# Gate/up with more seven-product k-pairs in each pair of chunks, token sums in smaller steps

## The chip, the cores and the metric

The kernel runs on one NeuronCore of a Trainium2 chip, as one launch. The metric is the time on the device in microseconds (us), as the median of several runs. A profiled execution of the same kernel gives the trace that the rows below come from. TensorE (PE) multiplies, VectorE (DVE) and ScalarE (ACT) do element work, SyncE (SP) issues the weight transfers, GpSimd (POOL) has little to do here.

## What is computed

The reference is a two-layer decoder trunk over 256 tokens of width 2048, in float32: a layer with dilated attention, a layer with sparse attention, and behind each a SwiGLU feed-forward. The change touches the first half of the feed-forward, in both layers.

```python
def swiglu(u, w_gu, w_down):
    gu = u @ w_gu
    return (jax.nn.silu(gu[..., :D_FF]) * gu[..., D_FF:]) @ w_down
# in reference(), per layer, D_FF = 5632:
x = x + rmsnorm(o, g[1])
x = x + rmsnorm(swiglu(rmsnorm(x, g[2]), ffn_w_gu[l], ffn_w_down[l]), g[3])
```

## The kernel before

**Splits.** TensorE multiplies numbers of reduced length, so that each float32 operand is cut into a high and a low part and a product takes three matmuls: high by high, low by high, high by low. `split_ap` makes the parts of a weight tile: ScalarE copies it to `hi` (L258), VectorE subtracts to get `lo` (L259). A weight unit is a tile of 128x1024, loaded by SyncE into `raw`.

**Gate/up.** The hidden width is done in 22 chunks, each with 8 units (one for each k-pair u, two blocks of 128 of the input width). Chunks go in 11 pairs, cp = 0 to 10. In pair 0 both chunks run side by side (`x_unit`, L425 to L427). In pairs 1 to 7 (`GU_PAIRS`) `gu_pair` runs them as a `Block7` (L465 to L467), in which some k-pairs, the "quads" (kind "S"), are computed with seven products instead of eight, a Strassen-like 2x2 scheme over two halves of the tokens, two k-blocks and two chunks. `_gu_quads` says which: u = 0 and 1 in even pairs, 0 to 2 in odd ones. Pairs 8 to 10 run chunk by chunk in the plain form. Two plain units of a k-pair take 24 matmuls, a quad 21.

A quad needs combined weights: of the first chunk's unit a and the second's b it takes a high and a low part of one half of b (`hl`, 128x512), T13 (two subtractions of 128x512, L274 and L275), T24 (two additions of 128x512 into the raw tile, L284 and L285), and splits of a, T13 and T24 of 128x1024. It also needs combined activations. `x_sums` makes them in the course of pair 0, for each u: `xw` adds high and low part (L1106), `sv` and `sx` (L1110 to L1116) are the four sums of a quad (`Sx`, for u < 3), `sv` and `ex` (L1121 to L1127) the differences for plain units within a Block7 (`Ex`, for u from 2 on).

**Evacuation.** When a pair is done, `evac` adds its accumulators (L509, L515), applies Silu and multiplies (L1159, L1160); for plain chunks `gu_evac` does it (L1088, L1090). Then `gu_split` transposes each hidden block f2 (L1068) and makes its high and low parts `hT` (L1072, L1073). Blocks f2 from 14 on (`DN_S`) have seven-product k-pairs in the down projection, and `s_parts` makes their four sums here, on ScalarE (`s` L1043, `hT` and `sp` L1059) and VectorE (`sv` L1046 to L1049, `hT` and `sp` L1060). Blocks 14 and 15 come from pair 7.

**What sets the order.** The program's order is the order of each engine's queue. `take` fetches the next unit: before it hands one out it issues loads and splits up to `st["look"]` units ahead, as long as `st["res"]` + 2 of the 48 SBUF pages (tiles of 128x1024) are free; where they aren't, the split comes when the unit is taken. Pages hold raw, hi, lo, X, the sums and the growing `hT`. The side work (`x_sums`, `gu_evac`, `sums`, `evac`) consists of generators that move on with the ticks of the products: `yield n` waits n ticks, and one plain unit gives 8 ticks.

```python
    def room(n):
        return len(pages.own) + len(pages.free) >= st["res"] + n
            # in take(), twice for each unit:
            if st["split"] < min(i + 1 + st["look"], n, ...) and room(2):
                split_one()
```

Of the kernel before, what the change touches and what calls it, by code (L numbers as in the profile page):

```python
# [18 lines left out]
S = 256  # L19
D = 2048  # L20
KT = D // P
HD = 128
DFF = 5632
FT = DFF // P
# [65 lines left out]

GU_PAIRS = range(1, 8)
GU_E = range(2, KT // 2)


def _gu_quads(cp):
    return tuple(range(2 + cp % 2))


def _gu_steps(cp):
# [5 lines left out]
def _gu_order(l):  # L107
    n, o = KT // 2, []
    for cp in range(FT // 4):
        if cp == 0:  # L110

            o += [(f"gu{l}", c * n + u) for u in range(n) for c in range(2)]
        elif cp in GU_PAIRS:
            o += _pair_order(f"gu{l}", n, cp, _gu_steps(cp))
        else:
            o += [(f"gu{l}", 2 * cp * n + u) for u in range(2 * n)]
    return o


# [100 lines left out]
def trunk(ctx: ExitStack, tc: tile.TileContext, a: dict, out: bass.AP):  # L220
# [858 lines left out]
    def gu_evac(f2, pts, H, rf, Sp):  # L1079

        while "r" not in rf:
            yield 0
        H.grow(f2)
        hs = []
        for t in range(2):
            r = rf["r"][:, t:t + 1]
            g = tmp.tile([P, S], F32, tag="ev1", name="ev1", bufs=2)
            nc.scalar.activation(g, pts[t][1][:, :S], AF.Silu, scale=r)  # L1088
            h = tmp.tile([P, S], F32, tag="ev2", name="ev2", bufs=2)
            nc.vector.scalar_tensor_tensor(h, pts[t][1][:, S:], r, g, op0=OP.mult, op1=OP.mult)  # L1090
            banks.put(pts[t][0])
            hs.append(h)
        yield 8
        yield from gu_split(f2, hs, H, Sp)

    def x_sums(X, Sx, Ex):

        e = None
        for u in range(KT // 2):
            while not X.done.issuperset((2 * u, 2 * u + 1)):  # L1100
                yield 0
            yield 6
            x = X.t[u][1].bitcast(F32)
            i, w = pages.get([P, 2, 2, P], F32, "xw")
            tt = nc.vector.tensor_tensor
            tt(out=w.rearrange("p k t q -> p k (t q)"), in0=x[:, :, 0, :], in1=x[:, :, 1, :], op=OP.add)  # L1106
            yield 2
            if u < 3:
                sv = tmp.tile([P, 4, P], F32, tag="sv", name="sv")
                tt(out=sv[:, 0], in0=w[:, 1, 1], in1=w[:, 0, 1], op=OP.add)  # L1110
                tt(out=sv[:, 1], in0=sv[:, 0], in1=w[:, 0, 0], op=OP.subtract)
                tt(out=sv[:, 2], in0=w[:, 0, 0], in1=w[:, 0, 1], op=OP.subtract)
                tt(out=sv[:, 3], in0=w[:, 1, 0], in1=sv[:, 1], op=OP.subtract)
                pg = pages.get([P, 4, 2, P], F32R, "sx")
                nc.scalar.activation(pg[1][:, :, 0, :], sv, AF.Copy)
                tt(out=pg[1][:, :, 1, :], in0=sv, in1=pg[1][:, :, 0, :].bitcast(F32), op=OP.subtract)  # L1116
                Sx[u] = {"pg": pg, "s": [[pg[1][:, j, k, :] for k in range(2)] for j in range(4)]}
                yield 2
            if u in GU_E:
                sv = tmp.tile([P, 4, P], F32, tag="sv", name="sv")  # L1120
                tt(out=sv[:, :2], in0=w[:, :, 0], in1=w[:, :, 1], op=OP.subtract)  # L1121
                at = (u - GU_E[0]) % 2 * 2
                if at == 0:
                    e = pages.get([P, 4, 2, P], F32R, "ex")
                    Ex[("pg", u)] = e
                nc.scalar.activation(e[1][:, at:at + 2, 0, :], sv[:, :2], AF.Copy)
                tt(out=e[1][:, at:at + 2, 1, :], in0=sv[:, :2], in1=e[1][:, at:at + 2, 0, :].bitcast(F32),  # L1127
                   op=OP.subtract)
                for k in range(2):
                    Ex[2 * u + k] = [e[1][:, at + k, j, :] for j in range(2)]  # L1130
            pages.put(i)

    def gu_pair(l, cp, X, Sx, Ex, H, Sp, rf):
# [12 lines left out]
        def evac():  # L1146
# [18 lines left out]
            for e in T["pg"]:  # L1165
                pages.put(e[0])

        for j, (kd, u) in enumerate(plan):
            blk.step(kd, u)
            if kd == "S" and all(e[0] != "S" for e in plan[j + 1:]):  # L1170
                spawn(sums())
        spawn(evac())

    def ffn(l, X, rf, gidx, step=lambda u: None, first=lambda c: None):
# [3 lines left out]
        spawn(x_sums(X, Sx, Ex))  # L1178
        for cp in range(FT // 4):
            if cp in GU_PAIRS:  # L1180
                st["res"], st["look"] = 5, 5
                gu_pair(l, cp, X, Sx, Ex, H, Sp, rf)
                continue
            if cp == GU_PAIRS[-1] + 1:
                st["spare"] = lambda: 2
                st["res"], st["look"] = 2, 4
                for e in Sx.values():
                    pages.put(e["pg"][0])
                for key, e in Ex.items():
                    if isinstance(key, tuple):  # L1190
                        pages.put(e[0])
            for fs in [(0, 1)] if cp == 0 else [(2 * cp,), (2 * cp + 1,)]:
                pts = [[bank(), bank()] for _ in fs]
                for u in range(KT // 2):
                    for p in pts:
                        x_unit(p, f"gu{l}", X, 2 * u, 512, u == 0, u == KT // 2 - 1, fs[0] == FT // 2 - 1)
                for f2, p in zip(fs, pts):
                    spawn(gu_evac(f2, p, H, rf, Sp))
        until(lambda: len(H.t) == FT // 2)
        X.release()  # L1200
        tail = Tail(gidx, "f")
        st["res"] = 4
# [92 lines left out]
    rf = {}  # L1295
# [412 lines left out]
```

## Time and profile before

| | |
|---|---|
| median of 3 runs | 2521.18 us (2521.03 to 2521.21) |
| profiled execution, time | 2519.93 us |
| its span | 2518.2 us |
| its mean granted clock of TensorE | 0.996 of full speed |
| gate/up, pairs 1 to 10, layer 1 | from about 1842 to 2284 us of the span |

A row of a timeline gives the start, the length, the engine, the line and what is written from what; the brackets at its end give the idle time of that engine just before and what ended it. Tiles stand without numbers there (`t` is T13). Matmuls are pipelined: a row's own length is longer than the distance to the next.

### The profile page before, as it was taken

To read this page: it belongs to the slowest core of one execution; us is meant where nothing else is said; L and a number is where in the kernel's file an instruction comes from. 1 tells how busy PE (TensorE), PEld (TensorE's weight loads), DVE (VectorE), ACT (ScalarE), POOL (GpSimd) and SP (SyncE) were. 2 spreads that over 40 slices of the span, in tenths; PEclk is the share of its full clock that TensorE was granted. 3 is DMA by queue.
4 is the path that set the end of the run, shared out by engine and by line. 5 is a ranking of instruction groups with operands and counts; after the bars stand their busy time and mean duration, and the time that the engine had idled before them with its cause. 6 is when DMAs were issued, how large, how long until landed. Compare 5 with 4: busy or idle time off the path is not lost. (4 is left out here: it accounts for less than half of the span.)

```text
span 2518.2 us, 32856 instructions
## 1 busy us (share of the span) xinstructions
PE 2478.4 (98%) x12122; PEld 2098.3 (83%) x12122; DVE 1859.0 (74%) x2638; ACT 1330.3 (53%) x1932; POOL 59.2 (2%) x74
## 2 busy tenths in 40 slices
PE   8999999999999999999999999999899999999998
PEld 7899999988788888888888888888778888888886
DVE  8565555557898878578897866896688987758796
ACT  7443444446555545455565566565455555545553
POOL 5000000000000000000000000000000000000000
PEclk9999999999999999999999999999999999999999
DMA  7555545576465546556586675346455655656664
GB/s 281 182 177 175 168 164 171 177 246 222 173 213 179 194 166 220 175 193 210 200 292 205 211 249 209 118 151 218 159 176 176 217 176 176 214 171 209 213 225 155
DMA packets 138529, 491.28 MB, mean 195 GB/s; under 512 B 15712, under 2 KB 15840, under 8 KB 138368
## 3 DMA queue, kind: packets, MB, share of 16 engines
q1 hardware_dynamic: 134208, 476.24, 55.4%
q0 software_dynamic: 3440, 11.83, 1.3%
q8 instruction: 95, 1.56, 0.3%
q10 hardware_dynamic: 720, 1.11, 0.1%
q14 instruction: 66, 0.54, 0.1%
HBM read 482.82 MB, written 6.29 MB: 194 GB/s over the span
## 5 line engine op out<-in xcount | busy, mean ns | idle before, releaser
L259 DVE TENSOR_TENSOR lo<-raw,hi 128x1024 fp32r<-128x1024 f32 (+2 forms) x899 | 1048.0, 1206 | 260.9 <-ACT hi L258 234.4
L258 ACT ACTIVATE hi<-raw 128x1024 fp32r<-128x1024 f32 (+2 forms) x899 | 889.7, 1035 | 153.2 <-PE bk L467 32.7
L390 PE MATMUL bk<-xT,hi 128*128 128x512 f32 x1104 | 399.2, 405 | 0.0
L392 PE MATMUL bk<-xT,lo 128*128 128x256 f32 x1035 | 289.8, 280 | 0.0
L390 PEld LDWEIGHTS bk<-xT,hi 128*128 128x128 f32 x1104 | 204.1, 188 | 39.9 <-issue 0.2
L465 PE MATMUL bk<-hi,hT 128*128 128x512 f32 x576 | 224.3, 389 | 0.0
L466 PE MATMUL bk<-hi,hT 128*128 128x512 f32 x576 | 224.1, 389 | 0.0
L467 PE MATMUL bk<-lo,hT 128*128 128x512 f32 x576 | 224.1, 389 | 0.0
L465 PE MATMUL bk<-hi,xf 128*128 128x512 f32 x564 | 222.4, 394 | 0.0
L467 PE MATMUL bk<-lo,xf 128*128 128x512 f32 x564 | 220.0, 390 | 0.0
L466 PE MATMUL bk<-hi,xf 128*128 128x512 f32 x564 | 219.9, 390 | 0.0
L427 PE MATMUL bk<-lo,xf 128*128 128x512 f32 x512 | 200.5, 392 | 3.2 <-DVE lo L259 3.2
L425 PE MATMUL bk<-hi,xf 128*128 128x512 f32 x512 | 202.5, 395 | 0.9 <-ACT xf L556 0.6
L426 PE MATMUL bk<-hi,xf 128*128 128x512 f32 x512 | 200.0, 391 | 0.0
L392 PEld LDWEIGHTS bk<-xT,lo 128*128 128x128 f32 x1035 | 195.5, 189 | 3.2
L258 ACT ACTIVATE hi<-t 128x1024 fp32r<-128x1024 f32 x68 | 72.3, 1063 | 192.6 <-DVE t L275 175.6
L465 PEld LDWEIGHTS bk<-hi,hT 128*128 128x128 f32 x576 | 108.1, 188 | 22.6
L467 PEld LDWEIGHTS bk<-lo,hT 128*128 128x128 f32 x576 | 108.1, 188 | 22.4
L466 PEld LDWEIGHTS bk<-hi,hT 128*128 128x128 f32 x576 | 108.1, 188 | 22.3
L467 PEld LDWEIGHTS bk<-lo,xf 128*128 128x128 f32 x564 | 106.0, 188 | 22.2
L465 PEld LDWEIGHTS bk<-hi,xf 128*128 128x128 f32 x564 | 106.2, 188 | 21.3
L466 PEld LDWEIGHTS bk<-hi,xf 128*128 128x128 f32 x564 | 106.3, 188 | 21.0
(301 smaller groups left out, 4210.0 us busy)
## 6 DMA issues: line engine op xcount, KB each, us to landing
raw<-in_gu SPq DMA_DIRECT2D x352, 512.0 KB, 4.1
raw<-in_dn SPq DMA_DIRECT2D x176, 512.0 KB, 4.3
raw<-in_a_qk SPq DMA_DIRECT2D x96, 512.0 KB, 3.3
raw<-in_a_v SPq DMA_DIRECT2D x64, 384.0 KB, 3.1
raw<-in_cw SPq DMA_DIRECT2D x32, 512.0 KB, 4.4
raw<-in_b_out SPq DMA_DIRECT2D x32, 512.0 KB, 3.8
raw<-in_a_out SPq DMA_DIRECT2D x24, 512.0 KB, 3.9
raw<-in_b_q SPq DMA_DIRECT2D x24, 512.0 KB, 3.3
```

The costliest lines, as they stand in the source:

```text
L258: nc.scalar.activation(hi, src, AF.Copy)
L259: nc.vector.tensor_tensor(out=lo, in0=src, in1=hi.bitcast(F32), op=OP.subtract)
L390: mm(pt[:, :], lhsT=hi[:, ks], rhs=X.hl(kt), start=first, stop=last)
L392: mm(pt[:, S:], lhsT=lo[:, ks], rhs=X.part(kt, 0), start=False, stop=False)
L425: mm(p[:, :w], lhsT=xh, rhs=u[0][1][:, ws], start=f, stop=False)
L426: mm(p[:, :w], lhsT=xl, rhs=u[0][1][:, ws], start=False, stop=False)
L427: mm(p[:, :w], lhsT=xh, rhs=u[1][1][:, ws], start=False, stop=l)
L465: mm(p, lhsT=xh, rhs=wh, start=f, stop=False)
L466: mm(p, lhsT=xl, rhs=wh, start=False, stop=False)
L467: mm(p, lhsT=xh, rhs=wl, start=False, stop=e)
```

## The change

`GU_PAIRS` now reaches to pair 10, with three quads in pairs 1 to 7 and two in pairs 8 to 10. The number of units that may be split ahead is 5 throughout; the pages held in reserve are 5 up to pair 7, then 4 and 3. `Sx[2]` is given back at pair 8. X, the sums and the differences are given back one by one inside pair 10; before, the sums and differences went at the start of pair 8. The steps of `x_sums` are drawn apart, `gu_evac` (pair 0 alone now) waits before its first step (1 tick for the first chunk, 17 for the second) and 14 instead of 8 ticks before the transposes. The last pair's evacuation falls into the start of the down projection.

```diff
@@ -90,12 +90,12 @@
 
 
 
-GU_PAIRS = range(1, 8)
+GU_PAIRS = range(1, 11)
 GU_E = range(2, KT // 2)
 
 
 def _gu_quads(cp):
-    return tuple(range(2 + cp % 2))
+    return tuple(range(3 if cp < 8 else 2))
 
 
 def _gu_steps(cp):
@@ -110,10 +110,8 @@
         if cp == 0:
 
             o += [(f"gu{l}", c * n + u) for u in range(n) for c in range(2)]
-        elif cp in GU_PAIRS:
+        else:
             o += _pair_order(f"gu{l}", n, cp, _gu_steps(cp))
-        else:
-            o += [(f"gu{l}", 2 * cp * n + u) for u in range(2 * n)]
     return o
 
 
@@ -1080,6 +1078,7 @@
 
         while "r" not in rf:
             yield 0
+        yield 1 + 16 * f2
         H.grow(f2)
         hs = []
         for t in range(2):
@@ -1090,7 +1089,7 @@
             nc.vector.scalar_tensor_tensor(h, pts[t][1][:, S:], r, g, op0=OP.mult, op1=OP.mult)
             banks.put(pts[t][0])
             hs.append(h)
-        yield 8
+        yield 14
         yield from gu_split(f2, hs, H, Sp)
 
     def x_sums(X, Sx, Ex):
@@ -1099,12 +1098,12 @@
         for u in range(KT // 2):
             while not X.done.issuperset((2 * u, 2 * u + 1)):
                 yield 0
-            yield 6
+            yield 4
             x = X.t[u][1].bitcast(F32)
             i, w = pages.get([P, 2, 2, P], F32, "xw")
             tt = nc.vector.tensor_tensor
             tt(out=w.rearrange("p k t q -> p k (t q)"), in0=x[:, :, 0, :], in1=x[:, :, 1, :], op=OP.add)
-            yield 2
+            yield 3
             if u < 3:
                 sv = tmp.tile([P, 4, P], F32, tag="sv", name="sv")
                 tt(out=sv[:, 0], in0=w[:, 1, 1], in1=w[:, 0, 1], op=OP.add)
@@ -1113,9 +1112,10 @@
                 tt(out=sv[:, 3], in0=w[:, 1, 0], in1=sv[:, 1], op=OP.subtract)
                 pg = pages.get([P, 4, 2, P], F32R, "sx")
                 nc.scalar.activation(pg[1][:, :, 0, :], sv, AF.Copy)
+                yield 3
                 tt(out=pg[1][:, :, 1, :], in0=sv, in1=pg[1][:, :, 0, :].bitcast(F32), op=OP.subtract)
                 Sx[u] = {"pg": pg, "s": [[pg[1][:, j, k, :] for k in range(2)] for j in range(4)]}
-                yield 2
+                yield 3
             if u in GU_E:
                 sv = tmp.tile([P, 4, P], F32, tag="sv", name="sv")
                 tt(out=sv[:, :2], in0=w[:, :, 0], in1=w[:, :, 1], op=OP.subtract)
@@ -1124,10 +1124,12 @@
                     e = pages.get([P, 4, 2, P], F32R, "ex")
                     Ex[("pg", u)] = e
                 nc.scalar.activation(e[1][:, at:at + 2, 0, :], sv[:, :2], AF.Copy)
+                yield 3
                 tt(out=e[1][:, at:at + 2, 1, :], in0=sv[:, :2], in1=e[1][:, at:at + 2, 0, :].bitcast(F32),
                    op=OP.subtract)
                 for k in range(2):
                     Ex[2 * u + k] = [e[1][:, at + k, j, :] for j in range(2)]
+                yield 3
             pages.put(i)
 
     def gu_pair(l, cp, X, Sx, Ex, H, Sp, rf):
@@ -1165,10 +1167,19 @@
             for e in T["pg"]:
                 pages.put(e[0])
 
+        st["res"], st["look"] = (5 if cp < 8 else 4 if cp == 8 else 3), 5
+        if cp == 8:
+            pages.put(Sx.pop(2)["pg"][0])
         for j, (kd, u) in enumerate(plan):
             blk.step(kd, u)
             if kd == "S" and all(e[0] != "S" for e in plan[j + 1:]):
                 spawn(sums())
+            if cp == GU_PAIRS[-1] and kd != "a":
+                X.drop_one(u)
+                if kd == "S":
+                    pages.put(Sx[u]["pg"][0])
+                elif u == KT // 2 - 1 or (u - GU_E[0]) % 2:
+                    pages.put(Ex[("pg", u - (u - GU_E[0]) % 2)][0])
         spawn(evac())
 
     def ffn(l, X, rf, gidx, step=lambda u: None, first=lambda c: None):
@@ -1178,25 +1189,15 @@
         spawn(x_sums(X, Sx, Ex))
         for cp in range(FT // 4):
             if cp in GU_PAIRS:
-                st["res"], st["look"] = 5, 5
                 gu_pair(l, cp, X, Sx, Ex, H, Sp, rf)
                 continue
-            if cp == GU_PAIRS[-1] + 1:
-                st["spare"] = lambda: 2
-                st["res"], st["look"] = 2, 4
-                for e in Sx.values():
-                    pages.put(e["pg"][0])
-                for key, e in Ex.items():
-                    if isinstance(key, tuple):
-                        pages.put(e[0])
-            for fs in [(0, 1)] if cp == 0 else [(2 * cp,), (2 * cp + 1,)]:
-                pts = [[bank(), bank()] for _ in fs]
-                for u in range(KT // 2):
-                    for p in pts:
-                        x_unit(p, f"gu{l}", X, 2 * u, 512, u == 0, u == KT // 2 - 1, fs[0] == FT // 2 - 1)
-                for f2, p in zip(fs, pts):
-                    spawn(gu_evac(f2, p, H, rf, Sp))
-        until(lambda: len(H.t) == FT // 2)
+            pts = [[bank(), bank()] for _ in range(2)]
+            for u in range(KT // 2):
+                for p in pts:
+                    x_unit(p, f"gu{l}", X, 2 * u, 512, u == 0, u == KT // 2 - 1)
+            for f2, p in enumerate(pts):
+                spawn(gu_evac(f2, p, H, rf, Sp))
+        st["spare"] = lambda: 2
         X.release()
         tail = Tail(gidx, "f")
         st["res"] = 4
```

In all, TensorE's instructions go from 11611 to 11557 in the program.

VectorE, layer 1, where the last plain chunks are computed. Before, behind the transposes of block 20 (`hT`), four `sv` and the `hT` and `sp` of its sums are followed by splits of plain units, of which several are already done:

```order
L259 TENSOR_TENSOR lo_3002_19492<-raw_2993_19430,hi_3001_19491 128x1024
L1073 TENSOR_TENSOR hT_3000_19473<-sk_506_19500,hT_3000_19473 128x2x256
L1046 TENSOR_TENSOR sv_19512<-sk_506_19500,s11_19510 128x128
L1047 TENSOR_TENSOR sv_19512<-sv_19512,sk_506_19500 128x128
L1048 TENSOR_TENSOR sv_19512<-sk_506_19500,s11_19510 128x128
L1049 TENSOR_TENSOR sv_19512<-sk_506_19500,sv_19512 128x128
L1060 TENSOR_TENSOR hT_3000_19473<-sv_19512,hT_3000_19473 128x128
L1060 TENSOR_TENSOR sp_2979_19345<-sv_19512,sp_2979_19345 128x128
L1060 TENSOR_TENSOR sp_3004_19517<-sv_19512,sp_3004_19517 128x2x128
L259 TENSOR_TENSOR lo_3006_19531<-raw_2996_19448,hi_3005_19530 128x1024
```

Now, at the entry of pair 10 in layer 1, the end of the second of two such chains (blocks 18 and 19), and then the splits of the pair's first quad:

```order
L1046 TENSOR_TENSOR sv_19697<-sk_521_19685,s11_19695 128x128
L1047 TENSOR_TENSOR sv_19697<-sk_521_19685,sv_19697 128x128
L1058 TENSOR_TENSOR hT_3070_19639<-sv_19697,hT_3070_19639 128x128
L1058 TENSOR_TENSOR sp_3073_19680<-sv_19697,sp_3073_19680 128x128
L1058 TENSOR_TENSOR sp_3074_19702<-sv_19697,sp_3074_19702 128x2x128
L257 TENSOR_TENSOR hl_3076_19724<-raw_3065_19598,hl_3076_19724 128x512
L272 TENSOR_TENSOR t13_3077_19727<-raw_3065_19598,raw_3062_19580 128x512
L273 TENSOR_TENSOR t13_3077_19727<-raw_3065_19598 128x512
L282 TENSOR_TENSOR raw_3062_19580<-t13_3077_19727,raw_3062_19580 128x512
L283 TENSOR_TENSOR raw_3062_19580<-raw_3062_19580 128x512
L257 TENSOR_TENSOR lo_3080_19737<-t13_3077_19727,hi_3079_19736 128x1024
L257 TENSOR_TENSOR lo_3082_19751<-raw_3062_19580,hi_3081_19750 128x1024
```

The splits that stand behind the sums (`hl`, T13, T24) were plain `lo` before, of units further ahead.

TensorE at the same two places. Before, behind the transposes come plain units whose parts (`hi_3014`, `lo_3015`) were split long ahead:

```order
L1068 MATMUL sk_509_19676<-cst_70,ev2_19652 128x128
L1068 MATMUL sk_509_19676<-cst_70,ev2_19656 128x128
L1068 MATMUL sk_509_19676<-cst_70,ev2_19652 128x128
L1068 MATMUL sk_509_19676<-cst_70,ev2_19656 128x128
L425 MATMUL bk_508_19639<-hi_3014_19584,xf_2400_15826 128x512
L426 MATMUL bk_508_19639<-hi_3014_19584,xf_2400_15826 128x512
L427 MATMUL bk_508_19639<-lo_3015_19585,xf_2400_15826 128x512
L425 MATMUL bk_507_19638<-hi_3014_19584,xf_2400_15826 128x512
L426 MATMUL bk_507_19638<-hi_3014_19584,xf_2400_15826 128x512
```

Now, from the tenth matmul behind the second transposes of pair 10, the last products of the quad's unit a, then those with `hl` and T13 (`hi_3079`, `lo_3080`):

```order
L463 MATMUL bk_522_19717<-hi_3071_19673,xf_2441_15921 128x512
L464 MATMUL bk_522_19717<-hi_3071_19673,xf_2441_15921 128x512
L465 MATMUL bk_522_19717<-lo_3072_19674,xf_2441_15921 128x512
L463 MATMUL bk_518_19600<-hi_3071_19673,xf_2441_15921 128x512
L464 MATMUL bk_518_19600<-hi_3071_19673,xf_2441_15921 128x512
L465 MATMUL bk_518_19600<-lo_3072_19674,xf_2441_15921 128x512
L463 MATMUL bk_523_19732<-hl_3076_19724,sx_2462_16105 128x512
L464 MATMUL bk_523_19732<-hl_3076_19724,sx_2462_16105 128x512
L465 MATMUL bk_523_19732<-hl_3076_19724,sx_2462_16105 128x512
L463 MATMUL bk_524_19742<-hi_3079_19736,sx_2462_16105 128x512
L464 MATMUL bk_524_19742<-hi_3079_19736,sx_2462_16105 128x512
L465 MATMUL bk_524_19742<-lo_3080_19737,sx_2462_16105 128x512
```

What TensorE takes here is what VectorE makes in the piece above.

ScalarE, layer 1, from pair 0 to pair 1, before: the splits of the first quad, the load of the Silu table and the first Silu.

```order
L258 ACTIVATE hl_2460_16242<-raw_2447_16157 128x512
L258 ACTIVATE hi_2463_16262<-t13_2461_16245 128x1024
L258 ACTIVATE hi_2465_16280<-raw_2442_16132 128x1024
L1088 ACT_TABLE_LOAD
L1088 ACTIVATE ev1_16301<-bk_415_15833,r_f_15974 128x256
L1088 ACTIVATE ev1_16305<-bk_416_15834,r_f_15974 128x256
```

Now:

```order
L1126 ACTIVATE ex_2503_16349<-sv_16347 128x2x128
L256 ACTIVATE hi_2504_16351<-t13_2500_16328 128x1024
L256 ACTIVATE hi_2506_16370<-raw_2482_16220 128x1024
L1126 ACTIVATE ex_2503_16349<-sv_16385 128x2x128
L1087 ACT_TABLE_LOAD
L1087 ACTIVATE ev1_16397<-bk_424_15929,r_f_16070 128x256
L1087 ACTIVATE ev1_16401<-bk_425_15930,r_f_16070 128x256
L1087 ACTIVATE ev1_16437<-bk_426_15931,r_f_16070 128x256
```

The last two steps of the differences (`ex`) have moved in among and behind the quad's splits, the last of them just ahead of the table load.

## Rows read from the trace of the kernel before

**Rows 1.** The page, part 1: busy us, share of span, instructions, by engine.

```profile
PE 2478.4 (98%) x12122; PEld 2098.3 (83%) x12122; DVE 1859.0 (74%) x2638; ACT 1330.3 (53%) x1932; POOL 59.2 (2%) x74
```

**Rows 2.** Waits of TensorE: tile, line, releaser, us in total, times, longest.

```profile
PE sk L1068 <- DVE ev L1090: 5.3, 1, 5.3
PE bk L427 <- DVE lo L259: 3.2, 6, 0.5
```

**Rows 3.** Windows, gate/up of layer 1: length, PE, PEld, DVE, ACT, POOL, clock.

```profile
1939.00:1981.50 42.50, 42.50 (x194) 35.21 (x193) 38.65 (x47) 23.64 (x29) 0.00 (x0) 1.00 0.58 194
...
2196.00:2240.00 44.00, 44.00 (x200) 36.44 (x199) 25.50 (x34) 21.34 (x28) 0.00 (x0) 1.00 0.49 168
```

**Rows 4.** Timeline of TensorE, layer 1, pair 7: start us, length us, instruction.

```profile
2128.79 0.39 PE L466 MATMUL bk<-hi,xf 128*128 128x512 f32 x1
...
2133.78 0.39 PE L467 MATMUL bk<-lo,xf 128*128 128x512 f32 x1
```

**Rows 5.** Timeline of TensorE, pair 0 of layer 0: idle before, releaser in brackets.

```profile
652.39 0.40 PE L426 MATMUL bk<-hi,xf 128*128 128x512 f32 x1
653.31 0.51 PE L427 MATMUL bk<-lo,xf 128*128 128x512 f32 x1 [0.53 <-DVE lo L259]
```

**Rows 6.** Timeline of all engines, from pair 0 to pair 1 of layer 1.

```profile
1838.55 0.43 DVE L1127 TENSOR_TENSOR ex<-sv,ex 128x256 fp32r<-128x256 f32 x1 [0.48 <-ACT ex L1126]
...
1841.76 0.39 PE L467 MATMUL bk<-lo,xf 128*128 128x512 f32 x1
...
1845.15 1.28 ACT L1088 ACT_TABLE_LOAD   x1
1845.16 1.23 DVE L259 TENSOR_TENSOR lo<-raw,hi 128x1024 fp32r<-128x1024 f32 x1
...
1846.95 0.88 DVE L1090 SCALAR_TENSOR_TENSOR ev<-bk,r_f,ev 128x256 f32<-128x256 f32 x2 [0.56 <-ACT ev L1088]
...
1847.49 1.29 PE L1068 MATMUL sk<-cst,ev 128*128 128x128 f32 x4 [5.35 <-DVE ev L1090]
```

**Rows 7.** VectorE by line and shape, layer 1's gate/up: count, busy us, mean ns.

```profile
L259 DVE TENSOR_TENSOR lo<-raw,hi 128x1024 fp32r<-128x1024 f32 x167 | 197.0, 1221 | 35.5 <-ACT hi L258 28.8 <-PE bk L426 5.0 <-issue 0.8
...
L284 DVE TENSOR_TENSOR raw<-t,raw 128x512 f32<-128x512 f32 x20 | 13.8, 692 | 0.7
```

**Rows 8.** ScalarE by line and shape, same stretch.

```profile
L258 ACT ACTIVATE hi<-t 128x1024 fp32r<-128x1024 f32 x20 | 21.2, 1062 | 60.9 <-DVE t L275 49.5 <-PE bk L467 8.7 <-issue 2.6
```

**Rows 9.** Timeline of all engines, chunk 16 of layer 1, behind pair 7's transposes.

```profile
2152.37 0.60 PE L1068 MATMUL sk<-cst,ut 128*128 128x128 f32 x4
...
2155.62 1.23 DVE L259 TENSOR_TENSOR lo<-raw,hi 128x1024 fp32r<-128x1024 f32 x1
...
2157.43 0.68 DVE L1073 TENSOR_TENSOR hT<-sk,hT 128x512 fp32r<-128x512 f32 x1
...
2159.59 0.79 DVE L1060 TENSOR_TENSOR sp<-sv,sp 128x128 fp32r<-128x128 f32 x2
```

**Rows 10.** Timeline of TensorE, entry of pair 7 of layer 1.

```profile
2109.95 0.60 PE L1068 MATMUL sk<-cst,ut 128*128 128x128 f32 x4
...
2115.64 0.39 PE L465 MATMUL bk<-hl,sx 128*128 128x512 f32 x1
...
2116.32 0.39 PE L465 MATMUL bk<-hi,sx 128*128 128x512 f32 x1
```

**Rows 11.** Timeline of all engines, third quad of pair 7.

```profile
2129.58 1.22 DVE L259 TENSOR_TENSOR lo<-t,hi 128x1024 fp32r<-128x1024 f32 x1
...
2131.74 0.39 PE L467 MATMUL bk<-lo,sx 128*128 128x512 f32 x1
```

**Rows 12.** Windows of three thin stretches of TensorE, columns as in rows 3.

```profile
1784.00:1788.00 4.00, 2.97 (x11) 2.14 (x12) 2.54 (x6) 0.95 (x2) 0.00 (x0) 0.77 0.99 333
1796.00:1800.00 4.00, 2.20 (x11) 1.89 (x12) 2.89 (x5) 1.70 (x6) 0.00 (x0) 1.00 0.39 129
1847.50:1849.50 2.00, 2.00 (x7) 1.60 (x8) 1.15 (x4) 1.47 (x3) 0.00 (x0) 0.50 0.00 0
```

## The prediction

> **What bounds the kernel now.** I read the page's busy shares first, then TensorE's waits, then windows over one layer's gate/up, and last the timelines at the places where the diff acts. TensorE is busy 98% of the span and VectorE 74% [rows 1], so time goes only by taking work from TensorE, and VectorE's slack is what pays for it. The two waits that the change can reach are one of 5.3 us, where transposes want the first pair's gated product, and six of about half a us, where a product wants a low part [rows 2]. Inside gate/up TensorE has no gap: a pair of chunks with three seven-product k-pairs ("quads") takes 42.5 us, with VectorE busy 38.65; in the last pairs, without quads, VectorE works 25.50 of 44.00 [rows 3]. In an average that looks like room for two more quads in each. Order within a pair is another matter, and it decides here.
>
> **What it removes.** A quad has seven products of three matmuls where the plain form has eight: 3 matmuls less. There are 9 more quads in a layer (one more in pairs 2, 4 and 6, two each in 8, 9 and 10), 18 in all, so 54 matmuls. One matmul follows another by 4.99 us over 22 steps, 0.227 us [rows 4]; a row's own 0.39 overlaps the next. 54 x 0.227 = **-12.2 us**. TensorE is never late in these stretches now, so all of it lies on the path.
>
> **Sums in smaller steps, layer 0.** In the first pair VectorE makes token sums between the splits, each step waiting for ScalarE, and six times the low part comes late: the start-to-start distance is 0.92 instead of 0.227 [rows 5]. 6 x 0.69 = 4.1. With a unit's sums spread over about 13 ticks instead of 8, VectorE has its time between; bounds 0 and -4.1, I take **-4.1**, because the 0.53 shown as idle is small beside the five ticks gained.
>
> **The step from pair 0 to pair 1, layer 1.** TensorE stood from 1842.0 to 1847.49; the multiplies that it wants (L1090) started at 1846.95, behind a low part begun at 1845.16, while the table load for Silu lay beside that low part on ScalarE [rows 6]. Afterwards the transposes stand 18 matmuls later, so TensorE wants them at 1842.0 + 4.1 = 1846.1. But one unit's sums (an add of 0.69 [rows 7], one of 128x256 and its low part, 0.43 each [rows 6]) now stand behind that low part, and the table load behind the last of ScalarE's sums. The low part ends 1.55 earlier, at 1846.4 - 1.55 = 1844.85; then 0.69 + 0.43 + 0.42 of ScalarE + 1.28 of load + 0.5 of Silu + 0.88 of multiplies gives 1849.05. The wait is 2.95 instead of 5.35: **-2.4 us**. Ends: 0, and -5.35 with the slow matmuls behind the gap gone too (2 us at half clock, 1.0 lost [rows 12]), -6.4.
> The load's row is 1.28 us and Silu follows at once [rows 6]. The Trainium skill, "ScalarE: Activation LUTs", section "What ACT_TABLE_LOAD costs", counts about 1.38 us of drain with each 1.28 of load; by it this wait would be 4.3, the gain 1.0 and the forecast 1.4 later. The row shows no drain, so I leave it out.
>
> **What the new quads cost.** A plain k-pair wants two low parts of VectorE, 2 x 1.22 [rows 7], under 5.46 us of matmuls. A quad wants three of 1.22 (T13, T24 and the first chunk's own) and five of 0.69 [rows 7], 7.1 us under 4.78 of matmuls. So its work must be done ahead, or quads must be rare. In pairs 1 to 7 three quads have the queue order that pairs 1, 3, 5 and 7 have now; the tightest place there is pair 7, where a low part ends at 2130.80 and is used at 2131.74 [rows 11]. 0.94 us stays, so I cost the extra quads in 2, 4 and 6 at nothing; cover lost there would cost up to 2 us for each pair, the amount by which a quad outlasts its own matmuls.
>
> In pairs 8 to 10 it is different, and this is the term that sets the sign. From the 15th hidden block on (f2 = 14) each block's evacuation also makes four sums for the down projection. This chain exists now, in the plain pairs: from the transposes at 2152.37 to the end of the last low part (2159.59 + 0.79) are **8.0 us**, one ordinary low part of 1.23 within [rows 9]. Nobody waits for it now, since four plain units were split ahead. In the changed kernel live pages (X, its sums, and a growing H) leave room for fewer units ahead, and the order shown above has the first quad's splits on VectorE and ScalarE behind this whole chain. Both queues are worked in order.
> When TensorE wants them is in the entry of pair 7: counted from the first transposes, the first chunk's half (hl) at 5.7 us, T13's high part at 6.4 [rows 10], its low part two matmuls later, 6.8; T24's high part at 7.7; the next unit at 9.1.
> Pair 10 of layer 1 in full: ScalarE gets to hl at 7.5 and is ready at 8.1: a wait of 2.4. VectorE's part of hl ends at 8.0 + 0.7 = 8.7, T13's two subtractions at 10.1, ScalarE's high part 1.06 later [rows 8], 11.15; wanted at 8.1 + 0.7 = 8.8: 2.35. The two additions for T24 stand ahead of T13's low part on VectorE: 10.1 + 1.4 + 1.2 = 12.7, wanted at 11.15 + 0.45: 1.1. Together 5.9. Then the two engines, lighter loaded for the rest of the pair, catch up.
> The same count for the others, by what their queues hold behind the chain: pair 9 has hl and the subtractions ahead in layer 1 (T13's high part 9.2 against 6.4, then a low part 1.75 late: 4.6), in layer 0 only the units before the quad (5.3); pair 8 has the whole first quad or all but T24 ahead (2.9 in each layer); pair 10 of layer 0 has not even the first plain unit split (8.1). Sum: 2.9 + 4.6 + 5.9 + 2.9 + 5.3 + 8.1 = **+29.7 us**. Ends: 0, by the row of pair 7, where splits stand behind transposes as well, though without the chain, and nobody waits [rows 11]; and 29.7 plus the clock's share below. I take 29.7, because the chain is itself a row of this stretch.
>
> **Start of the down projection.** The last pair's evacuation now meets its first units. Both ends open, 0 to +2; **+1** for one more chain beside splits that are late by less than one.
>
> **Sum.** -12.2 - 4.1 - 2.4 + 29.7 + 1.0 = +12.0. The profiled execution was 2519.93 us, 1.25 below the median of 2521.18; I set the sum on the median: **2533 us**.
>
> **Rivals.**
> A: VectorE keeps up. If the waits in pairs 8 to 10 don't come (the pages come free early enough, or the chain's pieces are too short to matter), only the gains remain: 2521.2 - 18.7 = 2502.5, and 2498 with all of layer 1's wait. For it: VectorE idles 18 us in each of these pairs [rows 3]. Against it: that idle time is at the other end of the pair, and the queue order puts the chain first.
> B: only pair 10 waits. Where part of the quad is split ahead, as in pairs 8 and 9, TensorE's own delay may give VectorE enough time; then the waits are 5.9 + 8.1 = 14.0 and the time 2521.2 - 18.7 + 14.0 + 1 = 2517.5, on the edge of what can be told from no change. It decides the sign at waits of 18 us: below, faster.
> C: the clock falls as well. After the 5.35 us wait TensorE ran two us at 0.50, 1.2 of 2.4 GHz [rows 12], losing 1.0; in another thin stretch, busy 2.97 of 4.00, the clock was 0.77, and in one busy 2.20 of 4.00 it stayed at 1.00 [rows 12]. If each of the six entries loses 1 to 2 us in this way: 2539 to 2545. The Trainium skill, "TensorE: Matmul & The Clock Gate", section "HAM oscillation", has it that gaps in which TensorE starves bring the slow clock back each time, and that the price is paid at every repetition; by it C would be the rule here. The rows say once yes and once no, and the entries hold matmuls between their waits.
>
> **Chances.** Forecast (2526 to 2538) 0.52; A (2498 to 2508) 0.14; B (2511 to 2526) 0.20; C (2538 to 2545) 0.14. The range 2508 to 2544 leaves out A and a little of C. About 0.2% (5 us) can be told from no change: below 2516 lie A and under half of B, 0.22; between 2516 and 2526 the rest of B and the forecast's edge, 0.14; above, 0.64.
>
> **What would show it.** In the trace of the changed kernel: TensorE's waits list should have products of gate/up (L463 to L465) waiting on ScalarE's and VectorE's splits (L256, L257), some 30 us, all within 10 us of the transposes that open pairs 8, 9 and 10, in both layers, largest in pair 10 of layer 0; the window of each such pair should last 44.0 - 1.4 + its wait. Pairs 2, 4 and 6 should take 42.4 without a wait. The six half-us waits of layer 0 should be gone, and the transposes of layer 1 wait near 3 us. If pairs 8 to 10 show no waits, my chain or its place in the queues is wrong, and the time is A's; if pair 7 or earlier waits, the cover of 0.94 was too thin.

## The result and the profile after

The changed kernel takes 2546.2 us (2545.09 to 2546.96, 4 runs), before 2521.14 us (2521.03 to 2521.21, 4 runs): ratio 1.0099, 95% interval 1.0082 to 1.0117. That is 25 us slower. The direction was forecast, the size was not: the forecast was 12 us slower, and the time lies 2 us above the range. Executions with a mean granted clock below 0.7, such as one of ten of e4_late, are left out of all numbers.

The profiled execution has a span of 2543.3 us, 25.1 more than before, at a mean clock of 0.992 instead of 0.996. TensorE's waits in it (tile, line, releaser, us in total, times, longest), to be held against [rows 2]; lines are two lower than before in this part of the kernel:

```profile
PE bk L463 <- ACT hi L256: 14.9, 8, 2.9
...
PE bk L465 <- DVE lo L257: 6.2, 10, 1.4
PE sk L1066 <- DVE ev L1089: 4.7, 2, 3.0
PE bk L463 <- ACT hl L256: 3.9, 2, 2.3
```

The waits on L427 of [rows 2] have gone but for one, the one at the transposes has become two, and 25.0 us in all on the splits of weights (L256, L257; 14.9, 6.2 and 3.9 above) are new. The windows tell where, against [rows 3]: pair 2 of layer 1 with three quads, then pairs 9 and 10 of layer 0, then 9 and 10 of layer 1.

```profile
1906.70:1949.10 42.40, 42.40 (x193) 35.13 (x192) 38.66 (x47) 23.64 (x29) 0.00 (x0) 1.00 0.57 195
1023.20:1074.30 51.10, 47.10 (x196) 37.39 (x195) 36.54 (x52) 23.25 (x32) 0.00 (x0) 0.93 0.45 151
1074.30:1126.90 52.60, 46.32 (x196) 36.31 (x195) 41.99 (x57) 28.63 (x37) 0.58 (x1) 0.97 0.58 202
2208.80:2259.10 50.30, 46.34 (x195) 37.23 (x194) 37.33 (x53) 24.48 (x33) 0.00 (x0) 0.93 0.45 154
2259.10:2310.40 51.30, 46.96 (x195) 37.35 (x194) 42.46 (x59) 28.06 (x37) 0.57 (x1) 0.93 0.59 205
```

Pair 2 takes 42.40 us without a gap, as a pair with three quads did before. The other four take 50 to 53 us, with TensorE idle for 4 to 6 of them and a clock of 0.93 to 0.97.

A pair is counted from the transposes that open it to those that open the next. With two quads it should take 43.1 us (42.4 with three, and 0.68 for the one saving less). The 44.0 - 1.4 of the prediction took the width of its window for the length of a plain pair; two plain chunks are 2 x 22.23 = 44.5. What the six pairs took above that, beside the wait that the prediction gave to each:

| pair | layer 0, forecast | measured | layer 1, forecast | measured |
|---|---|---|---|---|
| 8 | 2.9 | 46.2 - 43.1 = 3.1 | 2.9 | 47.7 - 43.1 = 4.6 |
| 9 | 5.3 | 51.1 - 43.1 = 8.0 | 4.6 | 50.3 - 43.1 = 7.2 |
| 10 | 8.1 | 52.6 - 43.1 = 9.5 | 5.9 | 51.3 - 43.1 = 8.2 |

Together 40.6 us where 29.7 were forecast. The entry of pair 10 of layer 1, which the prediction went through step by step, shows what is right in that count and what is missing (timeline of all engines; start, length, instruction, idle before and its releaser):

```profile
2259.10 0.60 PE L1066 MATMUL sk<-cst,ut 128*128 128x128 f32 x4
...
2266.37 0.79 DVE L1058 TENSOR_TENSOR sp<-sv,sp 128x128 fp32r<-128x128 f32 x2
2266.61 0.61 ACT L256 ACTIVATE hl<-raw 128x512 fp32r<-128x512 f32 x1
...
2267.28 0.50 PE L463 MATMUL bk<-hl,sx 128*128 128x512 f32 x1 [2.28 <-ACT hl L256]
...
2268.47 0.69 DVE L273 TENSOR_TENSOR t<-raw 128x512 f32<-128x512 f32 x1
...
2269.25 1.06 ACT L256 ACTIVATE hi<-t 128x1024 fp32r<-128x1024 f32 x1 [2.02 <-DVE t L273]
...
2270.36 0.80 PE L463 MATMUL bk<-hi,sx 128*128 128x512 f32 x1 [1.85 <-ACT hi L256]
2270.53 1.22 DVE L257 TENSOR_TENSOR lo<-t,hi 128x1024 fp32r<-128x1024 f32 x1
...
2271.80 0.80 PE L465 MATMUL bk<-lo,sx 128*128 128x512 f32 x1 [0.22 <-DVE lo L257]
```

Counted from the transposes at 2259.10, `hl` starts its product at 8.18 (forecast 8.1), T13's high part at 11.26 (11.15), its low part at 12.70 (12.7). The chain's last low part (L1058) ends at 8.06, for which the row of before gave 8.0 [rows 9]. So each of these products starts as forecast, within 0.1 us. Behind them comes what the sum left out. Windows of the same place, with the clock behind POOL's time:

```profile
2267.30:2272.40 5.10, 3.04 (x7) 1.48 (x8) 4.99 (x7) 2.76 (x3) 0.00 (x0) 0.74 0.00 0
2272.40:2276.60 4.20, 4.20 (x11) 3.33 (x10) 2.98 (x3) 1.92 (x3) 0.00 (x0) 0.51 0.50 162
2276.60:2310.40 33.80, 33.80 (x150) 27.93 (x149) 28.55 (x34) 18.59 (x22) 0.57 (x1) 1.00 0.74 260
```

In 2272.4 to 2276.6 TensorE is busy all the time, at 0.51 of full speed, the lower of its two levels (1.2 of 2.4 GHz; half clock from here on): 11 matmuls in 4.2 us, where 0.227 each would be 2.5. That is 1.7 us at this entry, beside some 0.7 among the waits; for all six, 40.6 - 29.7 = 10.9 us lie above the waits that were forecast.

### The profile page after: what moved, and what is told of

The parts are those of the page before. It is cut to its first block, busy times and chain, and to the rows that moved or that the text cites. A ratio compares the mean times of both kernels' runs of the same rounds, so it can differ in the third digit from the quotient of the medians.

```text
span 2543.3 us, 32987 instructions
## 1 busy us (share of the span) xinstructions
PE 2480.7 (98%) x12068; PEld 2095.1 (82%) x12068; DVE 1955.4 (77%) x2788; ACT 1359.8 (53%) x1974; POOL 61.8 (2%) x74
## 4 chain that ended last, share of the span: by engine, by line
PE 88%; DVE 7%; ACT 3%; issue 1%; DMA 1%; POOL 0%; SPq 0%; DVEq 0%; ACTq 0%; POOLq 0%
PE bk L465 16%; PE bk L463 16%; PE bk L464 16%; PE bk L388 12%; PE bk L390 6%; PE bk L424 5%; PE bk L425 5%; PE bk L423 5%; DVE lo L257 2%; ACT hi L256 1%; PE sk L1066 1%; PE sk L702 1%; PE bk L1387 1%; PE bk L1386 1%; DVE x L812 1%
## 5 line engine op out<-in xcount | busy, mean ns | idle before, releaser
L257 DVE TENSOR_TENSOR lo<-raw,hi 128x1024 fp32r<-128x1024 f32 (+2 forms) x899 | 1045.0, 1204 | 232.8 <-ACT hi L256 206.6
L256 ACT ACTIVATE hi<-raw 128x1024 fp32r<-128x1024 f32 (+2 forms) x899 | 888.5, 1035 | 141.9 <-PE bk L465 32.9
L463 PE MATMUL bk<-hi,xf 128*128 128x512 f32 x798 | 317.7, 398 | 5.3 <-ACT hi L256 5.3
L465 PE MATMUL bk<-lo,xf 128*128 128x512 f32 x798 | 314.3, 394 | 1.6 <-DVE lo L257 1.6
L464 PE MATMUL bk<-hi,xf 128*128 128x512 f32 x798 | 313.3, 393 | 0.0
L256 ACT ACTIVATE hi<-t 128x1024 fp32r<-128x1024 f32 x86 | 91.3, 1061 | 231.1 <-DVE t L273 212.4
L463 PEld LDWEIGHTS bk<-hi,xf 128*128 128x128 f32 x798 | 152.1, 191 | 36.7 <-ACT hi L256 6.6
L465 PEld LDWEIGHTS bk<-lo,xf 128*128 128x128 f32 x798 | 151.4, 190 | 35.0 <-DVE lo L257 2.9
L464 PEld LDWEIGHTS bk<-hi,xf 128*128 128x128 f32 x798 | 151.9, 190 | 30.7
L416 DVE TENSOR_TENSOR ev<-bk,ev 128x256 f32<-128x256 f32 x93 | 39.3, 422 | 91.7 <-ACT ev L415 91.0
L257 DVE TENSOR_TENSOR lo<-t,hi 128x1024 fp32r<-128x1024 f32 x86 | 104.8, 1218 | 3.6 <-PE bk L464 2.4
L415 ACT ACTIVATE ev<-bk 128x256 f32<-128x256 f32 x93 | 35.6, 382 | 130.5 <-PE bk L388 130.4
```

Source lines behind the costliest of these rows:

```text
L256: nc.scalar.activation(hi, src, AF.Copy)
L257: nc.vector.tensor_tensor(out=lo, in0=src, in1=hi.bitcast(F32), op=OP.subtract)
L415: nc.scalar.activation(t1, pt[1][:, S:], AF.Copy)
L416: nc.vector.tensor_tensor(out=t1, in0=pt[1][:, :S], in1=t1, op=OP.add)
L463: mm(p, lhsT=xh, rhs=wh, start=f, stop=False)
L464: mm(p, lhsT=xl, rhs=wh, start=False, stop=False)
```

## The experiments

### The edits one by one

**e1_quads.** The kernel before with

```diff
-    return tuple(range(2 + cp % 2))
+    return tuple(range(3))
```

> The kernel before with three quads instead of two in pairs 2, 4 and 6, nothing else. Theory (the early pairs have room, all of the loss is in pairs 8 to 10): 6 quads fewer matmuls, 18 x 0.227 = 4.1 us less than before, 2517.0, and no wait of TensorE in pairs 1 to 7. Rival (three quads in every pair in a row wear VectorE's lead down, so part of the loss is there): 2519 or more, with waits on L258 and L259 in pairs 3 to 7.

Measured 2516.87 us (ratio 0.9984, interval 0.9974 to 0.9994), with no new wait in pairs 1 to 7. The early pairs have the room that the prediction gave them: 4.1 us, the price of 18 matmuls.

**e2_spread.** The kernel before with `x_sums` of the changed kernel, and in `gu_evac`

```diff
+        if f2 < 2:
+            yield 1 + 16 * f2
         H.grow(f2)
...
-        yield 8
+        yield 14 if f2 < 2 else 8
```

> The kernel before with the new steps of x_sums and, for pair 0, the new waits of gu_evac; quads as before. Theory, from the changed kernel's trace (layer 0 is 4.0 us ahead and layer 1 1.8 us ahead by the end of pair 1): 5.8 us less than before, 2515.3; the six waits of 0.5 us gone, one of about 1.9 us at the transposes of layer 0 instead, and one of about 3.2 in layer 1. Rival (the smaller steps pay only together with more quads, since the sums of u = 2 are needed in every pair): within 1 us of before.

Measured 2514.56 us (0.9976, 0.9967 to 0.9986), 6.4 us less than before; the waits are those of the theory, two at the transposes (4.7 us together), and of the six one of 0.3.

**e3_both.** Both edits, pairs 8 to 10 plain.

> Both edits together: three quads in pairs 1 to 7, smaller steps, pairs 8 to 10 plain as in the kernel before. Theory: the parts add up, 2521.1 - 4.1 - 5.8 = 2511.2, and the 35 us to the changed kernel (less 8.2 us for its 12 further quads) stand in pairs 8 to 10 and the start of the down projection. Rival (part of the loss is in pairs 1 to 7 of the combination): 2514 or more.

Measured 2510.91 us (0.9962, 0.9948 to 0.9977). The parts add up. All of the loss arises in pairs 8 to 10 and what follows them: 2546.2 - 2510.9 = 35.3 us, and with it the 8.2 us that the 12 quads there take off TensorE.

### Is it the place of the quad behind the chain of sums?

**e4_late.** The changed kernel, quads of pairs 8 to 10 later:

```diff
+    if cp >= 8:
+        return a + _weave(b[:-1], q, 0) + b[-1:]
     return a[:3] + _weave(a[3:] + b[:-3], q, 0) + b[-3:]
```

> The changed kernel, but in pairs 8 to 10 the two quads come behind all six units of the first chunk instead of behind three; the same 27 quads per layer and the same work on every engine. Theory (the loss is the place of the first quad's splits behind the chain that makes the down projection's sums): the chain is over before TensorE gets to the quad, the waits go, and with the waits the half clock; 2521.1 - 12.2 - 5.8 + 2.4 at the start of the down projection = 2505.5. Rival (pages are too few or VectorE too slow in these pairs for quads anywhere): waits of the same size at the later place, 2535 to 2546.

Measured 2523.62 us (1.0008, 0.9999 to 1.0018; single runs from 2519.3 to 2526.8). The same work, 22.6 us less, and yet 18 above the theory. From transposes to transposes pairs 8 and 9 take 43.1 and 43.8 us in layer 0, 43.5 and 43.9 in layer 1: there the waits are gone, as the theory has it. Pair 10 still takes 51.7 and 48.9, and there the rival fits. In the timeline of pair 10 in layer 0 (lines two higher than in the changed kernel) it isn't a quad that waits:

```profile
1066.35 0.60 PE L1068 MATMUL sk<-cst,ut 128*128 128x128 f32 x4
...
1068.58 1.05 ACT L258 ACTIVATE hi<-raw 128x1024 fp32r<-128x1024 f32 x1
...
1069.66 1.23 DVE L259 TENSOR_TENSOR lo<-raw,hi 128x1024 fp32r<-128x1024 f32 x1
...
1071.53 1.05 PE L1068 MATMUL sk<-cst,ut 128*128 128x128 f32 x4
```

The high part begun at 1068.58 is that of a plain unit wanted at once: no unit is split ahead. By the rule of `take` that is so where too few pages of SBUF are free above the reserve; it is read from the kernel, and no run gave pair 10 more pages. On ScalarE it stands behind the transposed block's copies, its low part follows at 1069.66, and the second transposes come 5.2 us after the first instead of 1.8. Late quads cure pairs 8 and 9. In pair 10 the loss is not the place of the quads alone.

**e6_double.** The changed kernel; in `s_parts`

```diff
         tt(out=sv[:, 3], in0=A[:, 1, 0], in1=sv[:, 1], op=OP.subtract)
+        for _ in range(2):
+            tt(out=sv[:, 2], in0=A[:, 0, 0], in1=a21, op=OP.subtract)
+            tt(out=sv[:, 3], in0=A[:, 1, 0], in1=sv[:, 1], op=OP.subtract)
```

> The changed kernel with four of VectorE's 128x128 subtractions in the chain of the down projection's sums issued over again for each block (the same values are written again). They follow one another by 0.20 us, so 0.8 us for a block and 1.6 us for the two blocks at the entry of each of pairs 8, 9 and 10. Theory (the chain stands on the path there): about 1.6 us more at each of the six entries and some at the start of the down projection, 10 to 13 us in all, 2556 to 2559. Rival (TensorE waits there for pages or transfers, the chain only happens to be beside): 2546 to 2548.

Measured 2560.53 us (1.0158, 1.0141 to 1.0175), 14.3 above the changed kernel. The six pairs become 8.8 us longer in the profiled run (9.6 by 1.6 each), unevenly: 2.9, 0.9 and 1.5 in layer 0, 2.2, 0.9 and 0.5 in layer 1. The start of the down projection in layer 0 becomes 3.2 us longer. 1.8 arose at the entry of pair 1 in layer 0, which the edit doesn't touch: behind a wait of 1.7 us that both kernels have there, the clock fell to 0.51 in this run and not in that of the changed kernel. TensorE's waits on the same lines as in the changed kernel:

```profile
PE bk L463 <- ACT hi L256: 20.8, 9, 4.4
...
PE bk L463 <- ACT hl L256: 6.4, 2, 3.2
...
PE bk L465 <- DVE lo L257: 5.9, 10, 1.4
```

It is the waits on high parts, ScalarE's, that grew, from 14.9 to 20.8 and from 3.9 to 6.4: ScalarE waits for T13, and T13 for the chain.

**e7_double_before.** The same lines in the kernel before.

> The kernel before with the same four subtractions issued over again for each of 16 blocks. Theory (there the chain stands beside TensorE, with four plain units split ahead): within 1 us of before, 2521. Rival (VectorE has no room in pairs 8 to 10 in any form): 6 us or more above.

Measured 2521.4 us (1.0002, 0.9993 to 1.0011). With plain units split ahead the longer chain costs nothing; with quads behind it most of the added time counts, 8.8 of 9.6 us over the six pairs. The pair e6 and e7 shows that the chain is on the path in pairs 8 to 10 of the changed kernel, and was not before.

### Is the clock a cost of its own?

**e8_fill.** The changed kernel with added matmuls, by pair and product:

```diff
+FILL = {(0, 8): {"P7": 9, "P6": 3}, (0, 9): {"P1": 8, "P3": 9, "P5": 4}, (0, 10): {"P3": 6, "P5": 4},
+        (1, 8): {"P6": 12}, (1, 9): {"P3": 13, "P5": 6}, (1, 10): {"P1": 10, "P3": 9, "P5": 3}}
...
             f, e = self.n[key] == 1, self.n[key] == self.total[key]
+            for _ in range(self.fill.pop(key, 0) if f else 0):
+                mm(p, lhsT=xh, rhs=wh, start=True, stop=True)
```

> The changed kernel with 96 more matmuls (21.8 us at 0.227) put into the first quads of pairs 8 to 10, in the places where TensorE waits in the trace: each repeats the first matmul of a product whose accumulation has not begun, and the product then starts over. Nothing else moves. Theory (of the 40 us lost in the six entries about 28 are waits and about 11 are matmuls at half clock behind them): the added matmuls lie in the waits, the clock stays up, and the time falls by 5 to 10 us, to 2536 to 2541, though TensorE does 22 us more. Rival one (VectorE's lateness alone sets the time, the half clock is hidden in it): 2545 to 2547. Rival two (the waits are not where the trace puts them): up to 2568.

Measured 2538.14 us (1.0067, 1.0052 to 1.0082): 8.1 us less, with 21.8 us more of matmuls. The mean clock is back at 0.996. Pair 10 of layer 1 again, windows as above:

```profile
2260.00:2270.00 10.00, 9.88 (x41) 7.22 (x40) 9.70 (x14) 6.26 (x9) 0.00 (x0) 1.00 0.20 58
2270.00:2280.00 10.00, 10.00 (x46) 8.29 (x45) 8.22 (x10) 6.03 (x7) 0.00 (x0) 1.00 0.73 255
```

TensorE is busy 19.88 of 20 us at a clock of 1.00, where the changed kernel had idle time and then 0.51. By pair the gain is 2.6 (layer 0, pair 9), 1.6, 2.3 and 2.2 (layer 1, pairs 8, 9 and 10), and nothing in pair 8 of layer 0, where the clock had not fallen, or in pair 10 of layer 0, whose first wait was not filled. So the half clock is a cost beside the waits, not hidden in them, and the added matmuls lie within the waits. With the clock kept up, the five pairs other than pair 10 of layer 0 take 3.1 and 5.4 (layer 0), 3.0, 4.9 and 6.0 us (layer 1) above 43.1, where waits of 2.9, 5.3, 2.9, 4.6 and 5.9 were forecast: the waits alone were sized rightly.

### Towards a better kernel

**e9_tail.** Three quads in pairs 1 to 7 and the smaller steps; two late quads in pairs 8 and 9; pair 10 plain. The smaller steps are the edit of e2_spread, the late quads that of e4_late; the rest is

```diff
-GU_PAIRS = range(1, 8)
+GU_PAIRS = range(1, 10)
...
-    return tuple(range(2 + cp % 2))
+    return tuple(range(3 if cp < 8 else 2))
...
-                st["res"], st["look"] = 5, 5
+                st["res"], st["look"] = (5 if cp < 8 else 3), 5
```

> Smaller steps and three quads in pairs 1 to 7 as in the changed kernel; in pairs 8 and 9 two quads behind all six units of the first chunk; pair 10 in the plain form, with the sums' pages given back at its start as in the kernel before. Theory (late quads in pairs 8 and 9 cost almost no wait, and in pair 10 it was the want of pages): 2510.9 less 8 quads of 0.68 = 2505.5, and up to 2 us of short waits, 2505 to 2508. Rival (late quads cost as much as they save): 2511 or more.

Measured 2510.09 us (0.9957, 0.9942 to 0.9971; single runs 2508.1 to 2512.4), in between. The trace has 1.5 us of waiting for a high part of a plain unit at the entry of pair 9 in layer 0 and short waits elsewhere.

**e10_pages.** e9_tail with

```diff
-                st["res"], st["look"] = (5 if cp < 8 else 3), 5
+                st["res"], st["look"] = (5 if cp < 8 else 2), 5
+                if cp == 8:
+                    pages.put(Sx.pop(2)["pg"][0])
```

> e9_tail with one page more for the look-ahead in pairs 8 and 9: two instead of three pages held in reserve, and the sums of u = 2 given back at pair 8, where no quad uses them any more. Theory (what is left of the waits in pairs 8 and 9, 1.7 + 0.7 us at the entry of pair 9 in layer 0 and a few of 0.5, is want of pages): those waits go, 2 to 3 us less than e9_tail, 2506 to 2508. Rival (VectorE is late there for its own work): the same as e9_tail, 2508 to 2510.

A miss: 2513.12 us (0.9966, 0.9953 to 0.9979; single runs 2510.6 to 2514.0). The waits on splits went but for 0.5 us, and others came (lines four to five higher than in the changed kernel):

```profile
PE sk L1070 <- DVE ev L1094: 4.8, 2, 3.1
PE sk L1070 <- DVE ut L1167: 3.1, 3, 2.2
...
PE bk L469 <- DVE lo L261: 0.5, 2, 0.4
```

Of the 3.1 us at the transposes behind pairs 7 and 9 (`ut`), 2.7 are new. In pair 9 of layer 0 TensorE is 1.7 us ahead of e9_tail, but VectorE's multiplies begin no earlier (at 1065.99 us, in e9_tail at 1065.71), with a low part begun at 1061.85 just ahead of the adds, so that TensorE waits for the gated product instead.

That is not most of the difference. The span of the profiled run is 5.6 us longer than that of e9_tail (2511.9, 2506.3), and some 4.3 of that arises at half clock: 1.6 behind the new wait of 2.2 us, and 2.7 behind the 3.1 us at the first pair's transposes of layer 1, which both kernels have and the edit doesn't touch. The windows there, of e10_pages and then of e9_tail:

```profile
1846.10:1852.90 6.80, 6.27 (x17) 4.89 (x18) 5.71 (x9) 4.19 (x7) 0.00 (x0) 0.50 0.31 111
1846.00:1853.00 7.00, 7.00 (x35) 5.75 (x34) 6.69 (x10) 4.60 (x6) 0.00 (x0) 1.00 0.46 150
```

So what the freed pages of SBUF themselves cost or give is not shown.

**e11_evac.** e10_pages with `yield 26` instead of 14 ahead of the transposes of pair 0.

> e10_pages with the transposes of pair 0 set 26 instead of 14 ticks behind its gating, 12 ticks or 4.1 us later in TensorE's queue. Theory (TensorE waits there for VectorE's multiplies, 1.9 us in layer 0 and 3.2 in layer 1 with some matmuls at half clock behind it, and nobody needs the transposes early): both waits go, 5.1 us and 1 to 2 us of clock, 6 to 7 us less than e10_pages. Rival (the later transposes push VectorE's and ScalarE's hidden parts into the first quads of pair 1, and a wait of the same size comes there): no difference.

Measured 2506.23 us (0.994, 0.9925 to 0.9956), 6.9 less. Of the 4.8 us at the first pair's transposes 1.0 is left, and neither of those two stretches of half clock is there (mean clock 0.997, in e10_pages 0.995).

**e12_plain.** e3_both with that same `yield 26`.

> e3_both (plain pairs 8 to 10) with the transposes of pair 0 12 ticks later, as in e11_evac. Theory (the two waits behind pair 0 go here too): 2510.9 - 5.5 = 2505 to 2506, about where e11_evac is, which would say that the late quads of pairs 8 and 9 give back in waits what they save in products. Rival (the late quads pay 4 us): 2509 or more.

Measured 2505.35 us (0.9939, 0.9924 to 0.9954), as the theory has it: without any quad in pairs 8 to 10.

**e13_tail.** e11_evac, in `evac` of `gu_pair`:

```diff
-            yield 8
+            yield 8 if cp < 6 else 16
             for c in range(2):
```

> e11_evac with the transposes of pairs 6 to 9 set 16 instead of 8 ticks behind their gating. Theory (what e11_evac still waits for in pairs 7 to 9 are gated products that VectorE makes behind splits, 3.6 us in four places): those waits go, 2502 to 2504. Rival (the later transposes put the chain of the sums onto the quads of the next pair): no better than 2506, with waits on the splits instead.

Measured 2504.39 us (0.9935, 0.9918 to 0.9952; single runs 2503.9 to 2504.8, those of e12_plain 2505.3 to 2505.8). The waits at the transposes behind pairs 7 to 9 are gone; 2.1 us on splits, all in pair 9 (0.4 there in e11_evac), have come in their place. Of the 5.4 us that the 8 late quads save, 1.0 is left against e12_plain. This is the fastest kernel of the study, 16.4 us below before, and most of that needs no quad in pairs 8 to 10.

## Why the prediction was right in direction and wrong in size

- **54 matmuls, -12.2.** Right: e1 measured the 18 of pairs 2, 4 and 6 at 4.1 us.
- **Layer 0's sums, -4.1.** Right in sum: by the end of pair 1 the layer is 3.9 us ahead. Not by the steps given, so the sum is luck: each of the six units had lost 1.0 us (3.72 to 3.78 from one wait to the next, 12 matmuls are 2.72), not 0.69, and part of that went into a new wait that the prediction didn't have. TensorE now reaches the transposes before VectorE has its product (timeline of TensorE):

```profile
677.67 0.39 PE L465 MATMUL bk<-lo,xf 128*128 128x512 f32 x1
679.76 0.94 PE L1066 MATMUL sk<-cst,ev 128*128 128x128 f32 x4 [1.70 <-DVE ev L1089]
```

- **Layer 1's step to pair 1, -2.4.** The wait was foretold as 2.95 and is 3.04. The step itself gains 2.2, with half clock behind the wait as behind the longer one; 0.4 are lost ahead of it, in pair 0, where TensorE waits longer for `r_f` of GpSimd (1.3 us in two waits, before 1.0), so that 1.8 is left by the end of pair 1. The rows behind it, to be held against [rows 6]:

```profile
1857.22 1.22 DVE L257 TENSOR_TENSOR lo<-raw,hi 128x1024 fp32r<-128x1024 f32 x1
...
1858.88 0.39 PE L465 MATMUL bk<-lo,xf 128*128 128x512 f32 x1
...
1859.53 0.42 ACT L1126 ACTIVATE ex<-sv 128x256 fp32r<-128x256 f32 x1 [2.80 <-DVE sv L1121]
1859.96 1.28 ACT L1087 ACT_TABLE_LOAD   x1
...
1861.26 0.84 ACT L1087 ACTIVATE ev<-bk,r_f 128x256 f32<-128x256 f32 x2
1861.77 0.88 DVE L1089 SCALAR_TENSOR_TENSOR ev<-bk,r_f,ev 128x256 f32<-128x256 f32 x2 [1.36 <-ACT ev L1087]
...
1862.31 0.94 PE L1066 MATMUL sk<-cst,ev 128*128 128x128 f32 x4 [3.04 <-DVE ev L1089]
```

The sums' last high part (`ex`), the table load, Silu and the multiplies follow one another just as walked. That the wait comes out so near is luck in part: the 1.55 us by which the low part ahead of them was to end earlier stand on no row. Counted from the last matmul ahead of the old wait (1841.76) and its counterpart now (1854.80), it ends 1.0 us earlier, and the transposes start 0.5 us into the multiplies and don't wait for all 0.88 of them. The load takes 1.28 us and Silu starts 0.02 us after its end. The Trainium skill, "ScalarE: Activation LUTs", section "What ACT_TABLE_LOAD costs", would put 1.38 us of drain there; this trace doesn't show it either.
- **Nothing for the quads of pairs 1 to 7.** Right, e1 and e3.
- **The entries of pairs 8 to 10, +29.7.** The term that failed. Its waits were sized rightly, as the timeline above and e8 show, and the chain is on the path, as e6 with e7 shows; its size was 40.6, 10.9 more. The step at fault is that the sum priced the waits alone and put the half clock behind them at nothing: it was kept for a rival (C, chance 0.14), as an alternative to the forecast. It belonged into the sum: the rows showed half clock behind a wait [rows 12], and the forecast itself had two or three waits of 1 to 3 us in a row at each of six entries. e8, which kept the clock up at four of them, gives 8.1 us back. C's upper end, 2545, lies 1 us below the measured time. C's price of 1 to 2 us an entry was low too (10.9 over the five entries with half clock is 2.2 each): its row [rows 12] ends at 1849.5, and the clock stayed low for part of the next two us.

```profile
1849.50:1851.50 2.00, 2.00 (x9) 1.69 (x8) 0.65 (x2) 0.54 (x2) 0.00 (x0) 0.61 0.00 0
```

In pair 10 the chain ahead of the quad is not the whole of it: with late quads (e4) the pair still lost 8.6 and 5.8 us, on plain units not split ahead in layer 0, as the prediction had it there.

The Trainium skill, "TensorE: Matmul & The Clock Gate", section "HAM oscillation", says of a kernel with one long wait in each repetition that TensorE pays for the slow clock at every one. The trace agrees for five of the six entries (0.51 at the entry of pair 10 in layer 1); at pair 8 of layer 0, with waits of 2.00 and 0.53 us, the clock stayed at 1.00.

Nor is the half clock certain behind a given wait. Behind 1.7 us at the first pair's transposes of layer 0 the clock stayed at 1.00 in the changed kernel (680 to 684 us) and fell to 0.53 in e3_both (681.0 to 684.6); behind 3.1 us at those of layer 1 it stayed at 1.00 in e9_tail and fell to 0.50 in e10_pages.
- **Start of the down projection, +1.** It was 2.0 in layer 0 and 0.4 in layer 1, 2.4. In layer 0 a product waits for T13's low part, which stands behind the last pair's chain:

```profile
1136.60 0.40 PE L464 MATMUL bk<-hi,hT 128*128 128x512 f32 x1
1137.10 1.22 DVE L257 TENSOR_TENSOR lo<-t,hi 128x1024 fp32r<-128x1024 f32 x1
...
1138.37 0.51 PE L465 MATMUL bk<-lo,hT 128*128 128x512 f32 x1 [1.38 <-DVE lo L257]
```

The sum with what was measured: -12.2 - 3.9 - 1.8 + 40.6 + 2.4 = 25.1, the difference of the two spans. Of the 13.1 us by which the forecast of 12.0 fell short, 10.9 are the half clock's term, 1.4 the start of the down projection, 0.8 the two terms of the sums.

Rival A (VectorE keeps up) and B (only pair 10 waits) are out; what the prediction said against A, that VectorE's idle time is at the other end of the pair, is what e4 shows, where the quads were moved towards that end and the waits of pairs 8 and 9 went.

What stays open: e8's fill was not placed in pair 10 of layer 0, so that the clock's share there is only seen in the trace. Whether more free pages of SBUF would cure pair 10 was not tried. Why 1.0 of the 5.4 us of e13's late quads is left is seen only in part: from transposes to transposes its pairs 8 and 9 take 43.1, 45.5, 43.5 and 43.8 us, 3.5 above four times 43.1, with 2.1 us of waits on splits among them.

## What to carry to other kernels

A queue worked in order makes the place of idle time count more than its amount: VectorE was idle for 18 of 44 us in these pairs before, and an 8 us chain at their start still made the first quad of each late. Before work is taken off the busiest engine, look at what its supplier holds in its queue just ahead of the first use, and how many units are split ahead there. And when a sum forecasts repeated waits of 2 to 3 us for TensorE, price the half clock behind them as part of the sum, as a cost that most of them will have and not all.

## What was not expected of the hardware

That more work on TensorE can make a kernel faster: 96 added matmuls, 21.8 us by themselves, took 8.1 us off. At four of the six entries they filled idle time behind which the clock had fallen to 0.50 or 0.51, and the mean clock rose from 0.992 to 0.996.
